# Attention levels as diagonal blocks in column tiles, and head outputs stored as two parts

## The chip, the cores and the metric

One program runs on one core of a Trainium2 chip. The metric is the time of one execution in device microseconds (us), the median of several runs; shorter is better.

## What is computed

The program is one inference step of a two-layer trunk on 1024 latent and 128 context tokens of width 1024, all in float32. Layer 0 mixes tokens by gated linear attention (4 heads, key width 128, value width 256, forward and backward), layer 1 by a Fourier mixer; each layer ends in a gated MLP with a width-3 convolution. The change touches the attention of layer 0 and the projection behind it. What that computes, from the reference:

```python
bcum = jnp.cumsum(gi, axis=2)
diff = bcum[:, :, :, None, :] - bcum[:, :, None, :, :]
decay = jnp.exp(jnp.where(lower[:, :, None], diff, -jnp.inf))
attn = jnp.einsum('bhik,bhjk,bhijk->bhij', qi, ki, decay)
o = (jnp.einsum('bhij,bhjv->bhiv', attn, vi)
     + jnp.einsum('bhik,bhkv->bhiv', qi * jnp.exp(bcum), state))
...
o = rmsnorm(o, norm_g) * jax.nn.silu(r.reshape(B, L, GLA_HEADS, GLA_DV))
return o.reshape(B, L, GLA_V) @ w_o, s_f, s_b
```

The decay between tokens i and j depends on the key channel, so `attn` is no plain product of queries and keys.

## The kernel before

The 1152 tokens lie along the free dimension, channels on the partitions, in three column groups of 384 (`CH`); each group has three chunks of 128 tokens. For every head and every group, in the order 2, 1, 0, `attention` builds the 128x128 matrices `A` (`att`) of the three chunks. It goes through seven levels with half block sizes s = 64, 32, 16, 8, 4, 2, 1 (`LEVELS`). At a level, the pairs (i, j) in the same block of 2s tokens but in different halves get their decay as a product of two factors that refer to the middle of the block: GpSimd (L535) and VectorE (L537) subtract the reference, ScalarE takes the exponential (L540), GpSimd multiplies the keys (L541), VectorE the queries (L546), all into one tile `le` of a pool with four buffers (tag `m3`). TensorE then multiplies for each of the three chunks all 128 keys with all 128 queries (L549), and VectorE takes from the result only the pairs of the level, by a predicated copy under a mask (L551). The diagonal comes from a plain product (L527) that ScalarE copies into `A` with factor 2 (L528). A product of two float32 operands is issued as two MATMUL instructions, each with a weight load.

The weights' projections (`pq`, `pk`, `pv`, `pr`, `wo`) are split: every operand is a float32r part and a rest, three products each (L97 to L99). A scheduler of the framework sets the order on every engine, from priorities and its own costs. The projections of the next head, and for the last head the first half of the output projection, have lower priority and so fill TensorE between the levels. `tick` puts products of the background modulation (`mods`, L175) behind levels 0, 2, 4 and 6: 32 stationary columns, four products side by side in four column tiles of the array.

The normed and gated output `r` of a group is stored to memory for heads 0 to 2 (L590). In the last head `load_ot` loads those of heads 0 and 1 group by group into buffers of the tag `wr`, which has two and serves the weights too (L607), and `split_ot` makes the two parts (ScalarE L601, VectorE L602) in pages of the tag `u`, of which there are 14. `w_out((0, 1), X)` then multiplies them with the weights `wo00` to `wo03` (L97 to L99), for every pair of output blocks over groups, then blocks. Head 2 is loaded behind the attention, and `w_out((2, 3), ...)` follows.

Of the kernel before, what the change touches and what calls it, by code (L numbers as in the profile page):

```python
# [24 lines left out]
P = 128  # L25
# [5 lines left out]
CH = 384  # L31
# [14 lines left out]
def trunk(tc, a, o):  # L46
# [21 lines left out]
    def at_ps(name):  # L68
        return pp.tile([P, 512], F32, tag="at", bufs=4, name=name)
# [312 lines left out]
    convb = const("convb", [P, 2, NF], src=a["convb"])  # L382
    mask = const("mask", [P, len(LEVELS), P], U8)
    mraw = sb.tile([P, 1032], F32, tag="wr", bufs=2, name="mraw")
    nc.sync.dma_start(mraw[:, :len(LEVELS) * P], a["mask"])
    V.tensor_copy(mask.rearrange("p l i -> p (l i)"), mraw[:, :len(LEVELS) * P])
    for ch in range(NCH):
        ev_glr(ch, pss[ch])

    ot_dram = [dr.tile([2, P, T], F32, name=f"ot{h}") for h in range(3)]  # L390

# [87 lines left out]
    def kv(kt, v, c):  # L479
# [3 lines left out]
        return ps  # L483

    def attention(h, qk, pages):

# [22 lines left out]
        for cg in (2, 1, 0):  # L509
# [13 lines left out]
            att = t15("A")  # L523
            ps = at_ps("lv")
            for c in range(3):
                s = cg * CH + c * P
                PE.matmul(ps[:, c * P:(c + 1) * P], lhsT=qk[:, s:s + P], rhs=qk[:, T + s:T + s + P], start=True, stop=True)  # L527
            S.activation(att, ps[:, :CH], AF.Copy, scale=2.0)  # L528
            for li, s in enumerate(LEVELS):
# [13 lines left out]
                else:  # L543
                    S.activation(e[:, 1], e[:, 1], AF.Exp, scale=1.0 / TAU)
                    kk, kb = qk, base
                V.tensor_tensor(e[:, 1], e[:, 1], qk[:, T + base:T + base + CH], op=ALU.mult)  # L546
                ps = at_ps("lv")
                for c in range(3):
                    PE.matmul(ps[:, c * P:(c + 1) * P], lhsT=view(kk, kb + c * P, [1, P]),  # L549
                              rhs=e[:, 1, c * P:(c + 1) * P], start=True, stop=True)  # L550
                ins = V.copy_predicated(att.rearrange("p (c i) -> p c i", i=P),  # L551
                                  mask[:, li, None, :].to_broadcast([P, 3, P]),
                                  ps[:, :CH].rearrange("p (c i) -> p c i", i=P))
                if li % 2 == 0:
                    tick(1, behind=ins)
            qb = t30("qb")
            S.activation(qb, bb.rearrange("p (z i) -> p z i", z=2), AF.Exp, scale=1.0 / TAU)
# [31 lines left out]
            if h < 3:  # L589
                nc.sync.dma_start(ot_dram[h][:, :, cols(cg)].rearrange("d p t -> p d t"),  # L590
                                  r.rearrange("p (d t) -> p d t", d=2))
            yield
# [10 lines left out]

    def load_ot(*hs):
        for cg, h in ((cg, h) for cg in range(3) for h in hs):
            raw = sb.tile([P, 1032], F32, tag="wr", bufs=2, name="otr")[:, :2 * CH].rearrange("p (d t) -> p d t", d=2)
            nc.sync.dma_start(raw, ot_dram[h][:, :, cols(cg)].rearrange("d p t -> p d t"))  # L607
            for d in range(2):
                split_ot(h, d, cg, raw[:, d])

    def w_out(hs, X, after=None):
# [13 lines left out]
        if not after:  # L625
            for m2 in range(4):
                whl = weight(a["gwo"][0, m2], 1024, f"wo0{m2}")
                for ch in range(NCH):
                    for mi in range(2):
                        block(2 * m2 + mi, ch, whl, mi)  # L630
            return
# [21 lines left out]
    for h in range(H):  # L653
# [5 lines left out]
        if h < 3:  # L659
            with later(LQ):  # L660
                qk = gla_qk(h + 1)
                ahead = gla_gates_v(h + 1, pages)
        else:
            finish()
            load_ot(0, 1)
        for cg in range(3):
# [891 lines left out]
```

## Time and profile before

| | us |
|---|---|
| median of 3 runs | 2561.12 (2558.16 to 2563.42) |
| the profiled execution | 2564.86 |
| span of its trace, first to last instruction | 2563.0 |

The trace counts an engine as busy while one of its instructions runs; matmuls overlap, and their ends are modelled, so the mean duration of one is longer than the distance between two. PE is TensorE's matmuls, PEld its weight loads, DVE VectorE, ACT ScalarE, POOL GpSimd, SP the engine whose queue issues most transfers. PEclk is TensorE's granted clock as a share of 2.4 GHz. The attention of layer 0 with its output projection lies between about 115 and 730 us of the span.

### The profile page before, as it was taken

How to read it: one execution, taken by the hardware profiler on the slowest of the kernel's cores; microseconds unless marked ns; L12 is line 12 of the kernel's file. 1: busy time of each engine (PE TensorE's matmuls, PEld its weight loads, DVE VectorE, ACT ScalarE, POOL GpSimd, SP SyncE). 2: the span in 40 equal slices, each digit the busy share in tenths (PEclk: the TensorE clock that was granted, in tenths of full speed). 3: DMA queues.
4: the chain of work that ended last, by engine and by line, in shares of the span. 5: the costliest groups of instructions: out<-in, count | busy, mean ns of one | idle time of the engine just before them, and what ended most of it. 6: DMA issues, size and time to landing. Idle time of an engine off the chain costs nothing. (4 is left out here: it accounts for less than half of the span.)

```text
span 2563.0 us, 46543 instructions
## 1 busy us (share of the span) xinstructions
PE 2425.1 (95%) x18122; PEld 2329.2 (91%) x18122; DVE 1841.2 (72%) x3339; ACT 1089.3 (43%) x2086; POOL 730.9 (29%) x548
## 2 busy tenths in 40 slices
PE   5999999987999999999999998999899999999997
PEld 4998988877999999999999996998899999999997
DVE  7647475566699677777787877277987778778676
ACT  5435344445364323333345564344533333334553
POOL 3435454453202333444100005230144444410000
PEclk8999999998999999999999999999999999999999
DMA  7212222204233453232674357344223232267334
GB/s 263 69 54 89 80 80 82 67 21 146 87 116 124 132 172 104 91 96 83 212 248 135 112 153 216 107 156 144 90 87 117 83 96 87 80 229 224 93 86 125
DMA packets 200972, 309.85 MB, mean 121 GB/s; under 512 B 18288, under 2 KB 142064, under 8 KB 200752
## 3 DMA queue, kind: packets, MB, share of 16 engines
q1 hardware_dynamic: 196528, 302.66, 37.2%
q10 hardware_dynamic: 4224, 4.23, 0.5%
q8 instruction: 142, 2.33, 0.4%
q14 instruction: 78, 0.64, 0.1%
HBM read 233.71 MB, written 73.11 MB: 120 GB/s over the span
## 5 line engine op out<-in xcount | busy, mean ns | idle before, releaser
L98 PE MATMUL pd<-hl,wd 128*128 128x288 f32 x1112 | 328.7, 299 | 5.4 <-DVE hl L1085 5.2
L99 PE MATMUL pd<-hh,wd 128*128 128x288 f32 x1112 | 326.7, 297 | 0.0
L97 PE MATMUL pd<-hh,wd 128*128 128x288 f32 x1112 | 316.5, 298 | 5.5 <-ACT hh L1084 3.2
L809 POOL TENSOR_TENSOR s<-wa,s 128x512 fp32r<-128x512 f32 x114 | 157.0, 1377 | 278.6 <-ACT s L808 278.6
L1084 ACT ACTIVATE hh<-hr 128x288 fp32r<-128x288 f32 x308 | 133.2, 437 | 222.1 <-PE pd L98 213.3
L98 PEld LDWEIGHTS pd<-hl,wd 128*128 128x128 f32 x1112 | 210.8, 190 | 7.9 <-DVE hl L1085 7.4
L1085 DVE TENSOR_TENSOR hl<-hr,hh 128x288 fp32r<-128x288 f32 x308 | 138.5, 455 | 109.3 <-ACT hh L1084 108.7
L97 PEld LDWEIGHTS pd<-hh,wd 128*128 128x128 f32 x1112 | 204.2, 188 | 10.8 <-ACT hh L1084 5.7
L99 PEld LDWEIGHTS pd<-hh,wd 128*128 128x128 f32 x1112 | 210.4, 190 | 0.0
L809 POOL TENSOR_TENSOR a<-wa,a 128x512 fp32r<-128x512 f32 x76 | 100.1, 1318 | 334.7 <-ACT a L808 231.1
L808 ACT ACTIVATE s<-wa 128x512 fp32r<-128x512 f32 x120 | 75.5, 630 | 189.8 <-DVE wa L826 116.1
L977 ACT ACTIVATE hid<-hid 128x576 f32<-128x576 f32 x88 | 60.4, 686 | 161.5 <-DVE hid L972 102.0
L1074 DVE TENSOR_TENSOR wd<-wd,wd 128x512 fp32r<-128x512 f32 (+1 forms) x184 | 116.4, 642 | 9.7 <-ACT wd L1073 4.9
L808 ACT ACTIVATE a<-wa 128x512 fp32r<-128x512 f32 x80 | 50.3, 631 | 141.0 <-PE pa L99 76.2
L1073 ACT ACTIVATE wd<-wd 128x512 fp32r<-128x512 f32 (+1 forms) x184 | 104.4, 580 | 11.7 <-PE ps L99 4.0
L860 DVE TENSOR_TENSOR q<-q,ps 128x288 f32<-128x288 f32 x232 | 98.4, 444 | 10.1 <-PE ps L99 8.4
L535 POOL TENSOR_TENSOR le<-vbr 128x384 f32<-128x384 f32 x72 | 74.0, 1032 | 109.3 <-PE lv L549 95.5
L1208 POOL TENSOR_TENSOR fn<-fn 128x512 f32<-128x512 f32 x8 | 14.1, 1764 | 312.9 <-ACT wp L728 293.3
L541 POOL TENSOR_TENSOR le<-le,qk 128x384 f32<-128x384 f32 x72 | 91.6, 1278 | 35.6 <-ACT le L540 34.7
L97 PE MATMUL pa<-fh1x,a 128*128 128x288 f32 x320 | 95.3, 298 | 5.9 <-DVE c L860 3.6
L97 PE MATMUL ps<-fh1x,s 128*128 128x288 f32 x320 | 95.2, 298 | 3.0 <-DVE hid L917 3.0
L97 PE MATMUL ps<-fh0t,s 128*128 128x288 f32 x320 | 96.4, 302 | 1.4 <-DVE c L860 1.4
(689 smaller groups left out, 8852.5 us busy)
## 6 DMA issues: line engine op xcount, KB each, us to landing
hr<-hid SPq DMA_DIRECT2D x308, 144.0 KB, 2.2
wm<-in_wmod SPq DMA_DIRECT2D x112, 256.0 KB, 2.9
hid<-hid SPq DMA_DIRECT2D x44, 576.0 KB, 3.8
wa<-in_wup SPq DMA_DIRECT2D x40, 512.0 KB, 3.5
wg<-in_wup SPq DMA_DIRECT2D x40, 512.0 KB, 4.1
hid<-t SPq DMA_DIRECT2D x132, 144.0 KB, 3.3
wd<-in_wdn SPq DMA_DIRECT2D x16, 1024.0 KB, 8.0
wm<-in_wmod SPq DMA_DIRECT2D x96, 128.0 KB, 3.5
```

The source lines that it names most:

```text
L97: PE.matmul(ps, lhsT=wh, rhs=xh, start=first, stop=False, skip_group_check=skip)
L98: PE.matmul(ps, lhsT=wh, rhs=xl, start=False, stop=False, skip_group_check=skip)
L99: PE.matmul(ps, lhsT=wl, rhs=xh, start=False, stop=last, skip_group_check=skip)
L535: G.tensor_tensor(view(e, 0, [2 * s, nb], [s, 2], [1, s]), ref, view(bb, 0, [2 * s, nb], [CH + s, 2], [1, s]), op=ALU.subtract)
L541: G.tensor_tensor(e[:, 0], e[:, 0], qk[:, base:base + CH], op=ALU.mult)
L808: S.activation(w[name][:, :512], x, AF.Copy)
L809: (eng or G).tensor_tensor(w[name][:, 512:], x, w[name][:, :512].bitcast(F32), op=ALU.subtract)
L860: add.last = V.tensor_tensor(out[:, xs], x[:, xs], ps[s][:, :SUB], op=op)
L1073: S.activation(hi, x, AF.Copy)
L1074: low = V.tensor_tensor(lo, x, hi.bitcast(F32), op=ALU.subtract)
L1084: S.activation(hi[:, c], raw, AF.Copy)
L1085: V.tensor_tensor(lo[:, c], raw, hi[:, c].bitcast(F32), op=ALU.subtract)
```

## The change

Level 64 stays three full products, which ScalarE copies into `A`. Level 32 is computed only in diagonal blocks of 64, two column tiles a chunk; levels 16 to 1 and the diagonal only in diagonal blocks of 32, four column tiles a chunk (`diagonal`). Per column group that is 3 products of 128 columns, 6 of 64 and 72 of 32, in the place of 24 of 128. The products are issued in groups: level 64; levels 32, 16 and the diagonal; levels 8 and 4; levels 2 and 1. The blocks of 32 are gathered in a tile `near` of 96 columns by predicated copies, and four copies put it into `A`.

The outputs of heads 0 to 2 are split where they are made, over their values `v` and in place, and both parts are stored; `load_ot` loads a page of a head and half in one transfer from GpSimd's queue, without a split and without a buffer of `wr`. In the first `w_out` the loop over blocks is now outside that over groups.

```diff
--- before.py
+++ after.py
@@ -380,14 +380,18 @@
     gng = const("gng", [P, 2], src=a["gng"])
     convw = const("convw", [P, 2, 3, NF], src=a["convw"])
     convb = const("convb", [P, 2, NF], src=a["convb"])
-    mask = const("mask", [P, len(LEVELS), P], U8)
+
+    mask = const("mask", [P, len(LEVELS) - 2, 32], U8)
     mraw = sb.tile([P, 1032], F32, tag="wr", bufs=2, name="mraw")
     nc.sync.dma_start(mraw[:, :len(LEVELS) * P], a["mask"])
-    V.tensor_copy(mask.rearrange("p l i -> p (l i)"), mraw[:, :len(LEVELS) * P])
+    for g in range(4):
+        b = slice(32 * g, 32 * g + 32)
+        V.tensor_copy(mask[b], mraw[b, 2 * P:len(LEVELS) * P].rearrange("p (l i) -> p l i", i=P)[:, :, b])
     for ch in range(NCH):
         ev_glr(ch, pss[ch])
 
-    ot_dram = [dr.tile([2, P, T], F32, name=f"ot{h}") for h in range(3)]
+
+    ot_dram = [dr.tile([2, P, 2, T], F32, name=f"ot{h}") for h in range(3)]
 
     VV, BB, RR = slice(0, 2 * CH), slice(2 * CH, 4 * CH), slice(4 * CH, 6 * CH)
 
@@ -481,6 +485,14 @@
         PE.matmul(ps[:, :256], lhsT=kt[:, (c % 3) * P:(c % 3 + 1) * P], rhs=v[:, (c % 3) * 256:(c % 3 + 1) * 256],
                   start=True, stop=True)
         return ps
+
+    def diagonal(ps, n, kk, at, q):
+
+        for c in range(3):
+            for g in range(P // n):
+                PE.matmul(ps[n * g:n * g + n, c * n:(c + 1) * n], lhsT=view(kk, at + c * P + n * g, [1, n]),
+                          rhs=q[:, c * P + n * g:c * P + n * g + n], start=True, stop=True,
+                          **({} if n == P else dict(tile_position=(0, n * g))))
 
     def attention(h, qk, pages):
 
@@ -521,11 +533,9 @@
                     sbs[c - 1] = s_n
 
             att = t15("A")
-            ps = at_ps("lv")
-            for c in range(3):
-                s = cg * CH + c * P
-                PE.matmul(ps[:, c * P:(c + 1) * P], lhsT=qk[:, s:s + P], rhs=qk[:, T + s:T + s + P], start=True, stop=True)
-            S.activation(att, ps[:, :CH], AF.Copy, scale=2.0)
+            att3 = att.rearrange("p (c i) -> p c i", i=P)
+            near = sb.tile([P, 96], F32, tag="near", bufs=2, name="near")
+            todo = []
             for li, s in enumerate(LEVELS):
                 nb = CH // (2 * s)
                 base = cg * CH
@@ -543,16 +553,41 @@
                 else:
                     S.activation(e[:, 1], e[:, 1], AF.Exp, scale=1.0 / TAU)
                     kk, kb = qk, base
-                V.tensor_tensor(e[:, 1], e[:, 1], qk[:, T + base:T + base + CH], op=ALU.mult)
-                ps = at_ps("lv")
-                for c in range(3):
-                    PE.matmul(ps[:, c * P:(c + 1) * P], lhsT=view(kk, kb + c * P, [1, P]),
-                              rhs=e[:, 1, c * P:(c + 1) * P], start=True, stop=True)
-                ins = V.copy_predicated(att.rearrange("p (c i) -> p c i", i=P),
-                                  mask[:, li, None, :].to_broadcast([P, 3, P]),
-                                  ps[:, :CH].rearrange("p (c i) -> p c i", i=P))
+                made = V.tensor_tensor(e[:, 1], e[:, 1], qk[:, T + base:T + base + CH], op=ALU.mult)
+                todo.append((li, max(2 * s, 32), kk, kb, e[:, 1]))
+                ins = made
+                if li % 2 == 0:
+                    ps = at_ps("lv")
+                    at = 0
+                    with tc.issue_after(made.ins):
+                        for lj, n, kk, kb, q in todo:
+                            diagonal(ps[:, at:], n, kk, kb, q)
+                            at += 3 * n
+                        if li == 2:
+                            diagonal(ps[:, at:], 32, qk, base, qk[:, T + base:T + base + CH])
+                            S.activation(near, ps[:, at:at + 96], AF.Copy, scale=2.0)
+                    at = 0
+                    for lj, n, *_ in todo:
+                        src = ps[:, at:at + 3 * n].rearrange("p (c i) -> p c i", i=n)
+                        at += 3 * n
+                        if n == P:
+                            ins = S.activation(att3, src, AF.Copy)
+                        elif n == 64:
+                            S.activation(att3[:64, :, :64], src[:64], AF.Copy)
+                            ins = V.tensor_copy(att3[64:, :, 64:], src[64:])
+                        else:
+                            ins = V.copy_predicated(near.rearrange("p (c i) -> p c i", i=32),
+                                                    mask[:, lj - 2, None, :].to_broadcast([P, 3, 32]), src)
+                    todo = []
                 if li % 2 == 0:
                     tick(1, behind=ins)
+            for g in range(4):
+                b = slice(32 * g, 32 * g + 32)
+                src = near[b].rearrange("p (c i) -> p c i", i=32)
+                if g % 2:
+                    S.activation(att3[b, :, b], src, AF.Copy)
+                else:
+                    V.tensor_copy(att3[b, :, b], src)
             qb = t30("qb")
             S.activation(qb, bb.rearrange("p (z i) -> p z i", z=2), AF.Exp, scale=1.0 / TAU)
             V.tensor_tensor(qb, qb, view(qk, T + cg * CH, [0, 2], [1, CH]), op=ALU.mult)
@@ -587,8 +622,13 @@
                     V.tensor_tensor(o1, o1, rv, op=ALU.mult)
                     split_ot(3, d, cg, o1)
             if h < 3:
-                nc.sync.dma_start(ot_dram[h][:, :, cols(cg)].rearrange("d p t -> p d t"),
-                                  r.rearrange("p (d t) -> p d t", d=2))
+
+                hi = v.bitcast(F32R)
+                S.activation(hi, r, AF.Copy)
+                V.tensor_tensor(r.bitcast(F32R), r, hi.bitcast(F32), op=ALU.subtract)
+                for i, x in enumerate((v, r)):
+                    nc.sync.dma_start(ot_dram[h][:, :, i, cols(cg)].rearrange("d p t -> p d t"),
+                                      x.rearrange("p (d t) -> p d t", d=2))
             yield
 
     ots = {}
@@ -601,12 +641,10 @@
         S.activation(hi, src, AF.Copy)
         V.tensor_tensor(lo, src, hi.bitcast(F32), op=ALU.subtract)
 
-    def load_ot(*hs):
-        for cg, h in ((cg, h) for cg in range(3) for h in hs):
-            raw = sb.tile([P, 1032], F32, tag="wr", bufs=2, name="otr")[:, :2 * CH].rearrange("p (d t) -> p d t", d=2)
-            nc.sync.dma_start(raw, ot_dram[h][:, :, cols(cg)].rearrange("d p t -> p d t"))
-            for d in range(2):
-                split_ot(h, d, cg, raw[:, d])
+    def load_ot(h):
+        for d in range(2):
+            ots[h, d] = page(f"ot{h}{d}", F32R)
+            nc.gpsimd.dma_start(ots[h, d], ot_dram[h][d].rearrange("p i t -> p (i t)"))
 
     def w_out(hs, X, after=None):
         gate = vec(0, 2)
@@ -625,8 +663,8 @@
         if not after:
             for m2 in range(4):
                 whl = weight(a["gwo"][0, m2], 1024, f"wo0{m2}")
-                for ch in range(NCH):
-                    for mi in range(2):
+                for mi in range(2):
+                    for ch in range(NCH):
                         block(2 * m2 + mi, ch, whl, mi)
             return
         ws = []
@@ -662,7 +700,8 @@
                 ahead = gla_gates_v(h + 1, pages)
         else:
             finish()
-            load_ot(0, 1)
+            load_ot(0)
+            load_ot(1)
         for cg in range(3):
             next(att)
             if h < 3:
```

What this moves, at three places. In the rows, `lv` are the levels' results, `le` the factors, `mods` the background's, `pv` a projection of the next head; x3 is three like it.

TensorE, second column group of head 0, before, from the background's products behind level 16 to level 4 (the two rows x3 of `lv` are levels 8 and 4):

```order
L175 MATMUL mods_1856<-wm_1826,cs 32x128 x4
L175 MATMUL mods_1856<-wm_1828,cs 32x128 x4
L549 MATMUL lv<-le 128x128 x3
L98 MATMUL pv_1727<-wv10l,h_303 128x256
L99 MATMUL pv_1727<-wv10h,h_303 128x256
L97 MATMUL pv_1727<-wv10h,h_304 128x256
L98 MATMUL pv_1727<-wv10l,h_304 128x256
L99 MATMUL pv_1727<-wv10h,h_304 128x256
L97 MATMUL pv_1727<-wv10h,h_305 128x256
L549 MATMUL lv<-le 128x128 x3
L98 MATMUL pv_1727<-wv10l,h_305 128x256
```

and now, from level 64 to level 4 (the last row):

```order
L493 MATMUL lv<-le 128x128 x3
L493 MATMUL lv<-le 64x64 x6
L493 MATMUL lv<-le 32x32 x9
L186 MATMUL mods_1578<-sel,mrow_1891 128x8
L493 MATMUL lv<-le 32x32 x3
L493 MATMUL lv<-qk_689 32x32 x12
L493 MATMUL lv<-le 32x32
L175 MATMUL mods_1942<-wm_1887,cs 32x128 x4
L175 MATMUL mods_1942<-wm_1889,cs 32x128 x4
L493 MATMUL lv<-le 32x32 x11
L98 MATMUL pv_1792<-wv10l,h_303 128x256
L493 MATMUL lv<-le 32x32 x12
```

The products of levels 32 to 8 now stand together with the background's eight, one row of the projection `pv` stands between levels 8 and 4 where six stood, and a full product of the background (L186) stands inside level 16.

TensorE, last column group of the last head, with the output projection `wo` of heads 0 and 1 as the filling, before:

```order
L549 MATMUL lv<-le 128x128
L97 MATMUL wo_5503<-ot_5150,wo01h 128x384
L549 MATMUL lv<-le 128x128
L98 MATMUL wo_5503<-ot_5150,wo01h 128x384
L549 MATMUL lv<-le 128x128
L99 MATMUL wo_5503<-ot_5150,wo01l 128x384
L97 MATMUL wo_5503<-ot_5153,wo01h 128x384
L98 MATMUL wo_5503<-ot_5153,wo01h 128x384
L99 MATMUL wo_5503<-ot_5153,wo01l 128x384
L97 MATMUL wo_5524<-ot_5142,wo02h 128x384
```

and now:

```order
L493 MATMUL lv<-le 128x128 x3
L493 MATMUL lv<-le 64x64 x6
L493 MATMUL lv<-le 32x32 x11
L98 MATMUL wo_6204<-ot_5701,wo03h 128x384
L493 MATMUL lv<-le 32x32
L99 MATMUL wo_6204<-ot_5701,wo03l 128x384
L493 MATMUL lv<-qk_4264 32x32
L97 MATMUL wo_6204<-ot_5703,wo03h 128x384
L493 MATMUL lv<-qk_4264 32x32
L98 MATMUL wo_6204<-ot_5703,wo03h 128x384
L493 MATMUL lv<-qk_4264 32x32
L99 MATMUL wo_6204<-ot_5703,wo03l 128x384
```

Full products of a level alternated with the filling before; now products of a single 32-column tile do, one by one.

GpSimd, the last head's first two column groups (`ke` are the keys for the states, L87 the rest of a weight), before:

```order
L471 TENSOR_TENSOR ke<-ke,qk_3889 128x384
L87 TENSOR_TENSOR wr31l<-wr_4990,wr31h 128x1024
L471 TENSOR_TENSOR ke<-ke,qk_3889 128x384 x3
L535 TENSOR_TENSOR le<-vbr_4264 128x384 x2
L541 TENSOR_TENSOR le<-le,qk_3889 128x384 x2
L535 TENSOR_TENSOR le<-vbr_4558 128x384 x3
L541 TENSOR_TENSOR le<-le,qk_3889 128x384 x3
```

and now:

```order
L87 TENSOR_TENSOR wo01l<-wo_6014,wo01h 128x1024
L545 TENSOR_TENSOR le<-vbr_5057 128x384
L551 TENSOR_TENSOR le<-le,qk_4264 128x384
L647 DMA ot_5703<-ot_686 128x2304
L647 DMA ot_5705<-ot_687 128x2304
L87 TENSOR_TENSOR wo02l<-wo_6106,wo02h 128x1024
L647 DMA ot_5707<-ot_687 128x2304
L545 TENSOR_TENSOR le<-vbr_5057 128x384
L545 TENSOR_TENSOR le<-vbr_5368 128x384
L551 TENSOR_TENSOR le<-le,qk_4264 128x384 x2
```

The transfers of the pages `ot` stand in GpSimd's own order among the factors of the levels.

## Rows read from the trace of the kernel before

**Rows 1.** The page's first part: busy time, share, instructions

```profile
PE 2425.1 (95%) x18122; PEld 2329.2 (91%) x18122; DVE 1841.2 (72%) x3339; ACT 1089.3 (43%) x2086; POOL 730.9 (29%) x548
```

**Rows 2.** Busy time by stretch: stretch, length, engines (xcount), PEclk, DMA share, GB/s

```profile
115.60:257.00 141.40, 131.59 (x998) 119.66 (x995) 80.73 (x128) 59.40 (x104) 62.12 (x48) 1.00 0.26 80
...
594.00:616.00 22.00, 10.62 (x37) 8.88 (x36) 14.95 (x21) 13.72 (x22) 11.42 (x7) 0.61 0.58 206
616.00:730.00 114.00, 112.03 (x659) 109.73 (x658) 77.14 (x152) 38.09 (x69) 16.67 (x9) 0.99 0.30 106
```

**Rows 3.** Waits of PE, 115.6 to 534.8 us: total, times, longest

```profile
PE kt L474 <- POOL ke L471: 10.1, 9, 2.9
PE ov L577 <- DVE os L575: 5.5, 9, 1.6
PE mods L175 <- DMA wm<-in_wmod: 4.4, 3, 2.1
```

**Rows 4.** Waits of PE, 534.8 to 730 us

```profile
PE wo L97 <- ACT wo00h L86: 7.0, 1, 7.0
PE ov L577 <- DVE os L575: 6.5, 3, 2.9
PE o L565 <- DVE A L551: 2.5, 1, 2.5
PE wo L99 <- POOL wo00l L87: 1.4, 1, 1.4
```

**Rows 5.** Timeline, PE, 545 to 551 us: start, length, idle before it

```profile
545.20 2.84 PE L549 MATMUL lv<-le 128*128 128x128 f32 x24
549.94 0.91 PE L549 MATMUL lv<-le 128*128 128x128 f32 x6 [0.67 <-DVE le L546]
```

**Rows 6.** Timeline, PE, 130.9 to 136 us

```profile
131.00 0.65 PE L175 MATMUL mods<-wm,cs 128*32 128x128 f32 x16
...
134.93 0.28 PE L549 MATMUL lv<-le 128*128 128x128 f32 x1
135.13 0.42 PE L175 MATMUL mods<-wm,cs 128*32 128x128 f32 x8
135.49 0.44 PE L99 MATMUL pr<-h,wr00l 128*128 128x384 f32 x1
135.77 0.34 PE L97 MATMUL pr<-h,wr00h 128*128 128x384 f32 x1
135.94 0.33 PE L98 MATMUL pr<-h,wr00h 128*128 128x384 f32 x1
```

**Rows 7.** Line 175 alone, busy time by stretch of hundredths of a us

```profile
135.12:135.16 0.04, 0.03 (x4) 0.03 (x5) 1.00 0.00 0
135.16:135.26 0.10, 0.10 (x4) 0.10 (x8) 1.00 0.00 0
135.26:135.30 0.04, 0.04 (x8) 0.03 (x4) 1.00 1.75 410
```

**Rows 8.** Timeline, PE, end of the span: six products with 96 weight columns

```profile
2551.64 0.67 PE L256 MATMUL var<-mean,acc 128*96 128x2 f32 x6 [3.13 <-DVE acc L235]
```

**Rows 9.** Timeline, the other engines, 546 to 549 us

```profile
546.12 1.93 POOL L535 TENSOR_TENSOR le<-vbr 128x384 f32<-128x384 f32 x2 [7.84 <-PE lv L549]
547.45 0.84 ACT L540 ACTIVATE le<-le 128x768 f32<-128x768 f32 x1 [1.50 <-DVE le L537]
548.37 2.28 POOL L541 TENSOR_TENSOR le<-le,qk 128x384 f32<-128x384 f32 x2 [0.33 <-ACT le L540]
548.86 0.93 DVE L546 TENSOR_TENSOR le<-le,qk 128x384 f32<-128x384 f32 x1
```

**Rows 10.** Groups by line and shape, DVE, whole span: busy us, mean ns

```profile
L551 DVE COPY_PREDICATED A<-mask,lv 128x384 f32<-128x384 uint8 x84 | 49.2, 586 | 12.5 <-PE lv L549 7.5 <-ACT mrow L184 5.0
L624 DVE SCALAR_TENSOR_TENSOR x<-wo,modT,x 128x384 f32<-128x384 f32 x32 | 19.6, 614 | 16.7 <-PE wo L99 16.3 <-DMA x<-in_xT 0.3
L558 DVE TENSOR_TENSOR qb<-qb,qk 128x768 f32<-128x768 f32 x12 | 12.4, 1034 | 0.0
L602 DVE TENSOR_TENSOR ot<-otr,ot 128x384 fp32r<-128x384 f32 x18 | 11.0, 637 | 6.2 <-ACT ot L601 6.2
L624 DVE SCALAR_TENSOR_TENSOR x<-wo,modT,x 128x128 f32<-128x128 f32 x16 | 5.5, 343 | 0.0
```

**Rows 11.** Timeline, the norm of an attention output, 561 to 566 us

```profile
561.69 0.54 DVE L575 TENSOR_TENSOR os<-os,os 128x384 f32<-128x384 f32 x1
564.48 1.14 DVE L582 SCALAR_TENSOR_TENSOR o<-o,gng,os 128x384 f32<-128x384 f32 x2 [1.18 <-ACT os L579]
```

**Rows 12.** DMA issues, 520 to 740 us: KB each, median us to landing

```profile
x<-in_xT SPq DMA_DIRECT2D x4, 1152.0 KB, 8.6
```

## The prediction

> **What bounds the kernel now.** I read the busy shares first: TensorE 95%, VectorE 72%, the others under half [rows 1]. Then the busy time by stretch: in the attention TensorE works 131.6 of 141.4 us in the stretch of head 0, VectorE 80.7; only between 594 and 616 us TensorE rests, 10.6 busy of 22.0, at a granted clock of 0.61 [rows 2]. So TensorE's time is the stage's time, plus its waits. They come to about 25 us from 115.6 to 534.8 us, most of them for the keys of the states and for the norm [rows 3], and 18.9 us behind that, of which 8.4 are for the first weight of the output projection [rows 4]. The timelines show what a level costs and what it waits for [rows 5, 9], and what a change to column tiles and back costs, since the background's products already use them [rows 6, 7]. All sums are made against the profiled execution, 2564.9 us; the median of the three runs is 3.7 us lower.
>
> **Products of the levels.** Eighteen more level instructions take 2.84 - 0.91 us [rows 5], 0.107 each; a product is two, 0.214. A column group has 24: 5.15 us. Now it has 3 of these (0.64), 6 of 64 columns and 72 of 32. For 64 by 64 I take half the columns and two tiles side by side, 0.054: 0.32 us. For 32 by 32 the nearest row is the background, 32 weight columns but 128 moving: eight more instructions take 0.65 - 0.42 us [rows 6], 0.029 each, 0.058 a product. That is the upper end, and at it a group costs 5.14 us and nothing is saved. At the lower end only a quarter of the columns streams, 0.0145. The weights allow it: six loads of 96 columns with 2 moving ones take 0.67 us in all [rows 8], at most 0.037 us for 32 columns, and four tiles load side by side. Four products start within 0.04 us and no other in the next 0.10 [rows 7], so a start costs 0.01 at most and the 0.11 from four to four is streaming. I take 0.015: 1.08 us. A group then costs 2.04, saving 3.1; twelve groups (4 heads by 3) save **37.3**, ends 0 and 37.
>
> The Trainium skill (TensorE: Matmul & The Clock Gate, section "Wait — 56ns, not 53.3ns?") says that starts never come closer than about 25 ns however few columns there are. Taken across the tiles, 144 instructions would need 3.6 us a group, by estimate 30 us more over twelve groups; four starts in 0.04 us [rows 7] speak against it between tiles.
>
> **Changes of the array's mode.** From the last full product to the second projection row behind eight tiled ones it is 135.77 - 134.93 = 0.84 us; the work in it is 0.107, 8 by 0.029 and 0.17 (the distance 135.77 to 135.94) [rows 6]. The rest, **0.33 us**, is there and back: the array empties twice and loads weights without cover. I counted the runs of tiled products in TensorE's order up to the end of the output projection: 48 before, 183 now. Of the 135 more, 50 are in heads 0 to 2, and the last head has 75 that are one single level product between two rows of filling (the second place of the change). 135 by 0.33 is **44.6**. The ends are 0.30 and 0.37 a time, 40 and 50.
>
> No row shows a lone 32-column product. The Trainium skill (TensorEngine Tiling (Array Packing), section "Key Properties") has every change of tiling mode drain the array, however little is done between; by it single products pay like groups, and the sum is the one I make.
>
> Singles also lose the company of other tiles: 25 background products now stand alone, 0.214 for 0.058, 3.9 us; 75 level products take an estimated 0.06 for 0.015, 3.4; and eleven direct turns from 64 to 32 columns at half a trip are 1.9. Together **9.2**. TensorE's own work thus grows by 44.6 + 9.2 - 37.3 = **16.5**.
>
> **The chain of the levels.** Four buffers hold the factors, so those of level 4 start when level 64's products end: 545.20 + 0.91 = 546.11, GpSimd at 546.12; two subtractions, the exponential, GpSimd's and VectorE's products, and TensorE starts at 549.94, 3.8 us later, after 0.67 idle [rows 5, 9]. Without the predicated copies ahead of VectorE's part GpSimd bounds it: 1.93 + 1.14 + 0.3, 3.4 us. TensorE's work in between is now, for the first place shown: 6 by 0.054, 36 by 0.015, eight background products at 0.058, two trips, half a trip in, half a turn's worth from 64 to 32, and two full rows, about 2.5 us (2.0 to 2.8 over ten groups). So it waits 0.8 to 0.9 in each of ten groups; some 2 us of such waits exist now. **+6**, ends 0 and 13.
>
> **VectorE.** Seven predicated copies of 0.586 leave, 4.1 us a group. By the line through 0.614 at 384 and 0.343 at 128 columns, 0.31 stands for 96 and 0.41 for 192 [rows 10]: five copies, one of 192 and two of 96 are 2.6. Twelve groups save 18 us, 18 splits of 0.637 go (11.5), nine subtractions of 768 columns at 1.034 come (9.3). Twenty us less on an engine that TensorE waits for behind the norm and the state keys [rows 3]: I take **-4**, ends 0 and -12. ScalarE's changes (copies, nine more of 768 columns, 18 splits fewer) stay under its 43% and are set at nothing; were it the last to finish, nine copies of under 1 us would show. The nine more stores lie under a DMA share of 0.26 [rows 2]; the next head's state load queues behind them on SP, where VectorE has time.
>
> **The last head.** The loads leave the two `wr` buffers, so the weights no longer queue behind them: 7.0 + 1.4 go, and the wait of 2.5 for `A` too, as 19 rows of filling instead of 5 stand behind the last level of that group [rows 4]. A clock of 0.61 is 78% of that stretch at 1.2 GHz, some 8.2 of the 10.6 busy us; at 2.4 GHz they are 4.1 less [rows 2]. **-15**, ends 0 and -17.
>
> The filling of the first projection now ends with the last level of the last group. Before, that stretch is 112.0 of 114.0 us busy [rows 2]. The norm takes 561.69 to 565.62, 3.9 us, from its sum to its last product [rows 11], and gating and splitting about 1 more, with little beside it: **+5**, ends 0 and 8.
>
> **Sum:** 16.5 + 6 - 4 - 15 + 5 = +8.5, 2573.4 for a profiled execution, **2570** for the median.
>
> **The rivals.** A, faster: VectorE's queue is what TensorE's waits hang on. With 20 us less there, level 4 finds its factors (0 for +6), the waits for norm and state keys shrink by 12, the end is covered (0 for +5) and the last head gives 17: 16.5 - 12 - 17 = -12.5, **2549**. For it: VectorE is named in the wait before level 4 [rows 5]; against: GpSimd's three steps alone are 3.4 us. It decides when level 4 starts under 2.8 us behind level 64.
>
> B: small tiles run no faster than the background's, 0.058 a product: 37.3 more, less the 6 of the chain, **2601**. Against it stands the burst of four [rows 7]. The skill's floor between starts, named above, would come near this.
>
> C: the pages come late. Three wait for the last projections that read the old pages, and GpSimd and the levels queue behind their issue. Some 22 lone products with filling, 0.54 us each, cover 12 us, and the filling of the first page 5 more; a page of that size lands after 8.6 us [rows 12], three in turn after 26: 9 us of wait, **2579**.
>
> D: the lone products leave the array so idle that its clock falls to 1.2 GHz, as it did in the stretch at 0.61 [rows 2]. Some 75 times 0.23 us of array work doubles, 17 us, **2587**. Against it: runs of background products stand at a clock of 1.00 [rows 7].
>
> **How the numbers follow.** Forecast 0.48, A 0.24, C 0.13, D 0.08, B 0.07. Under 0.2%, 5 us, no measurement of this kernel tells a change. The forecast's terms spread it over 2558 to 2582: 0.30 slower, 0.16 same, 0.02 faster. A gives 0.20 faster and 0.04 same; C, D and B are slower. Together faster 0.22, same 0.20, slower 0.58. The range 2548 to 2590 leaves out B and the lower half of A.
>
> **What would show it.** Right: runs of tiled products with 0.2 us on either side, four 32-column instructions in about 0.03 us, alternating stretches in the last head of 0.5 to 0.6 us a step; a wait of 0.5 to 1.5 us before level 4; no wait for `wo00`; an idle gap before the second projection. Wrong: tiled products between full ones without the 0.33 us, or level 4 without a wait, would turn the sign; a wait on the loads of `ot` or a clock under 1 in the last head would add.

## The result, and the profile after

The changed kernel takes 2593.64 us (median of four runs, 2592.51 to 2601.66) against 2561.3 us; the ratio is 1.0134, interval 1.0111 to 1.0157. The forecast had the side right, 2570 us, and the loss nearly four times too small (8.9 us for 32.3); 2593.6 lies above the range. The profiled execution took 2601.66 us, 36.8 more than that of before; the stretches below are of these two executions. The page's first part now, as [rows 1]:

```profile
PE 2446.8 (94%) x19490; PEld 2317.3 (89%) x19490; DVE 1840.6 (71%) x3345; ACT 1096.0 (42%) x2123; POOL 736.9 (28%) x554
```

VectorE works as long as before, 1840.6 us for 1841.2, though some 20 us were reckoned to leave it. Where the time went is read from stretches cut at each head's first product of the projection `pr` and at the last of `wo` (columns as in [rows 2], which has head 0 before, 141.4 us). Before, heads 1, 2 and 3:

```profile
257.00:397.00 140.00, 133.09 (x1011) 120.51 (x1010) 79.59 (x127) 60.32 (x104) 64.00 (x50) 0.99 0.26 81
397.00:534.80 137.80, 128.61 (x942) 117.88 (x941) 78.93 (x127) 60.10 (x104) 60.50 (x46) 0.99 0.21 66
534.80:729.60 194.80, 175.89 (x1035) 167.83 (x1034) 132.94 (x237) 81.07 (x136) 56.62 (x42) 0.94 0.27 93
```

Now, heads 0 to 3:

```profile
115.10:263.70 148.60, 133.10 (x1337) 117.69 (x1334) 85.95 (x132) 63.82 (x119) 60.50 (x47) 0.94 0.27 84
263.70:409.70 146.00, 131.82 (x1353) 115.27 (x1352) 84.78 (x133) 64.39 (x119) 63.01 (x49) 0.98 0.29 86
409.70:553.40 143.70, 129.58 (x1293) 114.44 (x1291) 85.66 (x134) 64.26 (x117) 63.34 (x50) 0.98 0.24 73
553.40:764.90 211.50, 197.32 (x1373) 169.69 (x1372) 116.58 (x224) 74.43 (x129) 59.53 (x46) 0.96 0.29 102
```

These four hold 35.8 of the 36.8 us: 19.1 in heads 0 to 2, 16.7 in the last. In heads 0 to 2 TensorE stands idle 43.8 us instead of 25.9, and is busy 394.5 us instead of 393.3, more of it than before at the lower of its two clocks, 1.2 GHz: the granted clock is 0.94, 0.98 and 0.98 where it was 1.00, 0.99 and 0.99. Its waits in heads 0 to 2, for [rows 3]:

```profile
PE lv L493 <- DVE le L556: 12.5, 7, 2.4
PE kt L478 <- POOL ke L475: 9.4, 9, 1.7
PE mods L175 <- DVE modT L187: 7.7, 7, 1.8
PE ov L612 <- DVE os L610: 5.4, 9, 0.8
...
PE lv L493 <- POOL le L551: 1.3, 2, 0.7
```

The first, on the factors of a level, was this one before:

```profile
PE lv L549 <- DVE le L546: 1.1, 3, 0.5
```

The third, on `modT`, and the last are new; the second and fourth stayed. One group shows how they arise, TensorE first (the last row of the fence is level 4):

```profile
197.24 1.64 PE L493 MATMUL lv<-le 128*128 128x128 f32 x36
...
200.62 0.64 PE L175 MATMUL mods<-wm,cs 128*32 128x128 f32 x16 [1.03 <-DVE modT L187]
201.09 0.37 PE L493 MATMUL lv<-le 128*32 128x32 f32 x22
201.38 0.38 PE L98 MATMUL pv<-wv10l,h 128*128 128x256 f32 x1
203.35 0.40 PE L493 MATMUL lv<-le 128*32 128x32 f32 x24 [1.59 <-DVE le L556]
```

and VectorE and GpSimd in the same stretch:

```profile
198.18 2.31 DVE L547 TENSOR_TENSOR le<-vbr 128x384 f32<-128x384 f32 x2
200.42 0.15 DVE L187 TENSOR_TENSOR modT<-mods,bmod 128x8 f32<-128x8 f32 x1
200.49 1.44 DVE L547 TENSOR_TENSOR le<-vbr 128x384 f32<-128x384 f32 x1
201.85 1.36 DVE L556 TENSOR_TENSOR le<-le,qk 128x384 f32<-128x384 f32 x1
```

```profile
198.16 1.93 POOL L545 TENSOR_TENSOR le<-vbr 128x384 f32<-128x384 f32 x2 [3.50 <-PE lv L493]
200.41 2.39 POOL L551 TENSOR_TENSOR le<-le,qk 128x384 f32<-128x384 f32 x2 [0.33 <-ACT le L550]
```

Level 4 starts 203.35 - 197.24 = 6.11 us after level 64's first product; before it was 549.94 - 545.20 = 4.74 [rows 5], and 4.74 in the group shown here as well. Two things stretch it: level 1's subtraction (1.44) stands ahead of level 4's query product, and VectorE's instructions run long exactly while GpSimd's do, 1.36 us where 0.93 stood [rows 9].

A run of tiled products is what stands between two full ones, and a trip the change from full to tiled products and back. In the last head single products alternate with the filling (timeline; a row of filling by itself is 0.17 from the next [rows 6]):

```profile
602.36 0.25 PE L493 MATMUL lv<-le 128*32 128x32 f32 x2
602.54 0.44 PE L98 MATMUL pr<-h,wr31h 128*128 128x384 f32 x1
602.91 0.25 PE L493 MATMUL lv<-le 128*32 128x32 f32 x2
603.08 0.44 PE L99 MATMUL pr<-h,wr31l 128*128 128x384 f32 x1
```

A period is 603.08 - 602.54 = 0.54 us, so a trip costs about 0.35: the period less the 0.17, and less some 0.015 for the product itself.

### The profile page after: what moved, and what is told of

Same layout as the page of the kernel before. It is cut to its first block, busy times and chain, and to the rows that moved or that the text cites. A ratio compares the mean times of both kernels' runs of the same rounds, so it can differ in the third digit from the quotient of the medians.

```text
span 2599.9 us, 49329 instructions
## 1 busy us (share of the span) xinstructions
PE 2446.8 (94%) x19490; PEld 2317.3 (89%) x19490; DVE 1840.6 (71%) x3345; ACT 1096.0 (42%) x2123; POOL 736.9 (28%) x554
## 3 DMA queue, kind: packets, MB, share of 16 engines
q1 hardware_dynamic: 196528, 302.66, 36.8%
## 5 line engine op out<-in xcount | busy, mean ns | idle before, releaser
L899 DVE TENSOR_TENSOR c<-q,pa 128x288 f32<-128x288 f32 x80 | 36.0, 450 | 89.1 <-PE pa L99 85.6
```

The lines of the kernel that those rows point to most:

```text
L899: add.last = V.tensor_tensor(out[:, xs], x[:, xs], ps[s][:, :SUB], op=op)
```

## The experiments

**The two parts apart.** The changed kernel with the old stores, `load_ot` and loop of `w_out`:

```diff
-            load_ot(0)
-            load_ot(1)
+            load_ot(0, 1)
```

> Only the levels are changed; outputs of heads are stored, loaded and split as before, with the old loop order in the first output projection. Theory (the levels carry the loss: trips, the wait before level 4, the wait on modT, the clock): slower than before by 25 to 40 us, with the stretch of each of the heads 0 to 2 still 6 to 7 us longer than before. Rival (the pages that come late are what was missed): slower than before by only 5 to 15 us.

2603.3 us, ratio 1.0165 (1.015 to 1.018), 41.6 us slower than before: slightly above the theory. With the outputs as well (2593.64) it is 9.7 less. And the outputs alone, on the old levels:

> Only the outputs of heads 0 to 2 are changed (two parts, six page loads on GpSimd's queue, other loop order); levels as before. Theory, by my sum (the weights no longer queue behind the loads): faster than before by 5 to 15 us, the waits of 7.0 and 1.4 us for wo00 gone. Rival (late pages): 0 to 10 us slower, with waits for a page ot in their place.

2556.83 us, ratio 0.9982 (0.9968 to 0.9995): a gain of 4.8 us, just under the theory's lower end. The waits for `wo00` are gone, but in the last stretch (191.2 us for 194.8) others stand there:

```profile
PE kt L474 <- POOL ke L471: 5.3, 3, 3.0
PE wo L97 <- ACT vbr L449: 3.9, 1, 3.9
```

The loss is the levels'.

**Late filling.**

```diff
-                with later(LV):
+                with later(2400):
                     w_out((0, 1), X)
```

> The changed kernel with a lower priority for the first output projection, so that the level products of the last head stand in groups: 51 runs of tiled products fewer in TensorE's order. Theory (0.30 us a trip): 13 to 18 us faster than the changed kernel. Rival (alternating costs little, the filling is missed later): within 5 us of the changed kernel, or slower.

2588.95 us, ratio 1.01 (1.0073 to 1.0127): 4.7 less by the medians, as the rival had it, but 13.0 by the profiled executions. The last stretch is 199.2 us instead of 211.5. TensorE is busy 180.6 us there instead of 197.3, 0.33 us less for each of the 51 runs, and waits 4.4 us more. The price of a trip is borne out; the total does not decide between the two.

**VectorE's order.**

```diff
+                with tc.issue_after(mades[li - 2].ins) if li > 4 else ExitStack():
```

around the subtraction of line 547, `mades` being the list of the levels' `made`.

> The changed kernel with VectorE's subtraction of levels 2 and 1 held behind its query product of two levels before, so level 1's subtraction no longer stands ahead of level 4's product. Theory (VectorE's order makes the wait before level 4): level 4 starts about 4.2 us behind level 64's last product instead of 5.56 in the groups of heads 0 to 2, that wait falls from 12.5 us in all to under 4, and the kernel is 8 to 16 us faster than the changed one, the low clock behind that wait included. Rival (GpSimd's pace or the shared access of GpSimd and VectorE sets it): the wait stays over 10 us or moves to levels 2 and 1, the time within 4 us of the changed kernel.

2586.87 us, ratio 1.011 (1.0083 to 1.0137), 6.8 less; heads 0 to 2 fell by 13.1 us (145.4, 141.8, 138.0). Of these, 9.6 are TensorE's busy time (384.9 us for 394.5, with the clock at 0.96, 1.00 and 0.99) and only 3.5 its idle time. The same group's rows:

```profile
197.67 1.63 PE L493 MATMUL lv<-le 128*128 128x128 f32 x36
...
202.41 0.42 PE L493 MATMUL lv<-le 128*32 128x32 f32 x24 [0.52 <-DVE le L557]
```

Level 4 starts 4.74 us behind level 64, the old distance to the hundredth. The theory holds for that distance and nearly for the waits before the levels (5.1 us in all now, for under 4); the gain of the kernel stayed under its 8 us; the waits on GpSimd's factors rose from 1.3 to 3.9 us.

**Each wait taken away by itself moves.** A bank for the background's result:

```diff
-                pt = ps[:, P:P + 8]
+                pt = at_ps("modt")[:, :8]
```

> The changed kernel, with the background's small transposed result in a bank of its own, so that the next background products no longer wait until VectorE has read it. Theory (these waits are a loss of their own): the 7.7 us of waits on modT in heads 0 to 2 are gone, 11 runs of tiled products fewer save 3 us more, and the kernel is 7 to 12 us faster than the changed one. Rival (VectorE paces the levels anyway): the time goes into the wait before level 4, which stands right behind; within 4 us of the changed kernel.

2623.09 us, ratio 1.0237 (1.0195 to 1.028): a miss, worse than either theory. The waits on `modT` are gone and those before the levels more than doubled; levels 32 to 4 now stand in one piece, the row of filling ahead of level 4 gone:

```profile
PE lv L493 <- DVE le L556: 29.8, 15, 2.9
```

> The three repairs together: late filling, VectorE's order, a bank for the background's result. Theory (each loss stands for itself): gains add up, 4.7 + 6.8 + about 8 us against the changed kernel, about 2574 us. Rival (they share one cause, VectorE's queue): no more than the larger two, 2582 us or above.

2615.13 us (1.0199, 1.0156 to 1.0242): nothing adds up while the bank is in it.

**Fewer trips.** Each group's tiled products in two runs:

```diff
-                if li % 2 == 0:
+                if li in (0, 3, 6):
...
+                        todo = [todo[2], todo[3], todo[1], todo[0]]
...
+                        with tc.issue_after(lead.ins) if lead else ExitStack():
```

> The changed kernel with each column group's tiled products in two runs: levels 32, 16, 8 and the diagonal, and levels 4, 2 and 1, the last level's factors first in each, and the background's products beside them; VectorE's order and the late filling as in the experiments before. The runs of tiled products up to the end of the output projection fall from 183 to about 55. Theory (a trip costs 0.30 us wherever it stands): the time from full to tiled products and back falls by about 35 us, the stage is shorter than in the kernel before, the kernel at 2550 to 2568 us. Rival (what counts is the chain of the factors; with level 1's first, TensorE waits longer in one piece): waits before the second run of 2 us or more a group take most of it back, 2575 to 2595 us.

2588.66 us (1.0099, 1.0063 to 1.0134), as the rival had it. Head 0 took 138.3 us, under the 141.4 of before, heads 1 and 2 took 150.9 and 149.4. The products end together, so what hangs on the last comes late:

```profile
PE o L610 <- DVE A L600: 18.8, 9, 3.5
PE kt L478 <- POOL ke L475: 15.1, 9, 5.7
```

Then level 64 ahead of the states' keys, so that the chain starts early:

```diff
-            kt = khat(qk, bb, 1, cg)
...
+                if li == 1:
+                    kt = khat(qk, bb, 1, cg)
```

> The changed kernel, with level 64 of a group computed ahead of the keys for the states, so that its buffer comes free early and the factors of level 4 are made under the projection; in TensorE's order level 64 stands dozens of rows ahead of level 32. 30 runs of tiled products fewer as well. Theory (the loss of heads 0 to 2 is the chain of the factors behind level 64, with the clock that falls in its waits): waits before level 4 fall from 12.5 us to under 4, the stretches of heads 0 to 2 come to 141 us or less each, and the kernel is 15 to 25 us faster than the changed one. Rival (any wait removed comes back before the next level, since VectorE and GpSimd slow each other down): less than 8 us faster.

2601.79 us (1.0125, 1.0092 to 1.0159): no gain. With the order and the late filling:

> The same with VectorE's order and the late filling: 88 runs of tiled products fewer than in the changed kernel. Theory (chain and trips are separate losses): 2555 to 2568 us. Rival (they are the same loss): no better than the kernel with level 64 first alone, within 4 us of it.

2587.08 us (1.0085, 1.0058 to 1.0111). With two runs a group:

> Level 64 first, and the tiled products in two runs a group. Theory (with the chain out of the way the streaming that the tiles save is left over, 9 us a head by the accounts of the two-run kernel): 2540 to 2560 us. Rival (the second run waits for level 1 and the copies of A wait for it, as in the two-run kernel): 2570 to 2590 us.

2577.24 us (1.0048, 1.0034 to 1.0063), as the rival had it, 18.4 us of it in waits for the states' keys from GpSimd. Removing trips and placing levels helps, but GpSimd's and VectorE's work comes late wherever TensorE is sent.

**VectorE alone.** The key halves of levels 4 and 2 on VectorE (level 1 has none); `True` for `s <= 4` moves all:

```diff
-                    G.tensor_tensor(e[:, 0], e[:, 0], qk[:, base:base + CH], op=ALU.mult)
+                    (V if s <= 4 else G).tensor_tensor(e[:, 0], e[:, 0], qk[:, base:base + CH], op=ALU.mult)
```

and the same on line 545.

> The changed kernel with the key halves of levels 4 and 2 (subtraction and product) on VectorE instead of GpSimd. Theory (the two engines slow each other: a subtraction or product of VectorE takes 0.55 us without GpSimd's work beside it and about 1.0 to 1.2 with it): though VectorE has four more instructions a group, its subtractions fall from a mean of 0.97 us towards 0.8, level 4 starts 4.0 to 4.8 us behind level 64 instead of 5.56, and the kernel is 4 to 12 us faster than the changed one. Rival (VectorE's load is what counts): level 4 starts later than now, the kernel is 5 to 15 us slower.

2595.39 us (1.0123, 1.0092 to 1.0154), no gain, though the waits before the levels fell to 2.3 us in heads 0 to 2; 14.1 stand at the states' keys, 5.3 at `kv` and 7.4 at the copies of `A`. On the kernel with level 64 first and two runs:

> Level 64 first and two runs a group, with the key halves of levels 4 and 2 on VectorE. Theory: GpSimd's keys for the states come earlier too, their waits fall from 18.4 us to under 10, the time to 2560 to 2570 us. Rival: 2577 us or more, as without it.

2586.77 us (1.0095, 1.007 to 1.012), 9.5 slower than without: a miss. All levels:

> The same with all levels' key halves on VectorE, GpSimd only making the keys for the states. Theory (the slowing of each other is most of what GpSimd's share saves): VectorE's mean for a subtraction and a product falls to about 0.6 us, the waits for the keys of the states nearly go, the time 2550 to 2570 us. Rival (VectorE becomes the bound of the attention): heads 0 to 2 take 150 us or more each, 2590 us or above.

2558.13 us (0.9971, 0.9952 to 0.999), as the theory had it. On the old levels, half and all:

> The outputs in two parts with the old full-width levels, and the key halves of levels 4 and 2 on VectorE. Theory (the waits for the keys of the states, 6.4 us in heads 0 to 2, hang on GpSimd's queue): 3 to 6 us faster than the outputs alone, about 2552 us. Rival (with the predicated copies of 0.59 us VectorE has no room): slower than the outputs alone by 3 to 10 us.

> Outputs in two parts, the old full-width levels, all levels' key halves on VectorE: what the tiles are worth when VectorE has the work alone. Theory (the predicated copies of 384 columns leave VectorE no room): 5 us or more slower than the outputs alone, so that the diagonal blocks pay only here. Rival (GpSimd's help is worth nothing with the old levels either): as fast as the outputs alone or faster, 2545 to 2557 us.

2578.93 us (1.006, 1.0036 to 1.0083) and 2559.97 us (0.9998, 0.9985 to 1.0011), against 2556.83 for the outputs alone, 22 and 3 us slower: the first is worse than its rival, the second under its theory's 5 us. Full-width levels gain nothing from it. The states' keys on VectorE as well (line 475, `G` to `V`), beside level 64 first and two runs:

> Level 64 first, two runs a group, all levels on VectorE, and the keys for the states on VectorE too. Theory (the 17.3 us of waits for these keys come from GpSimd, whose queue holds weight splits of 2.4 to 3.0 us ahead of them): these waits fall under 8 us, the time is 4 to 10 us less than with the keys on GpSimd, about 2550 us. Rival (VectorE is full now): within 3 us of it or slower.

2546.52 us (0.9939, 0.9923 to 0.9954): faster than both kernels. The waits for the keys fell less than hoped, from 13.9 to 8.8 us in heads 0 to 2.

**The changed kernel, VectorE alone, nothing else:**

> The changed kernel with all levels' key halves on VectorE and nothing else. It has 34 runs of tiled products more in its order than the changed kernel, most of them single products in the last head. Theory (meeting of VectorE and GpSimd makes the waits of heads 0 to 2): each of these heads takes 5 us or more less than in the changed kernel, level 4 starts under 4.5 us behind level 64, the time is 8 to 20 us less, the trips of the last head excepted. Rival (two runs and level 64 first made the gain of the run before): within 5 us of the changed kernel or slower.

2590.71 us (1.0107, 1.0083 to 1.013). The total is that of the rival and hides two opposite moves:

```profile
116.90:255.50 138.60, 130.46 (x1334) 114.51 (x1331) 79.59 (x161) 60.52 (x111) 15.80 (x9) 0.96 0.27 85
255.50:393.30 137.80, 129.32 (x1352) 114.37 (x1351) 88.31 (x170) 64.25 (x120) 22.92 (x13) 0.98 0.29 91
393.30:527.80 134.50, 126.38 (x1288) 111.78 (x1287) 86.83 (x170) 64.08 (x119) 22.80 (x13) 0.99 0.24 78
527.80:756.20 228.40, 212.30 (x1379) 173.97 (x1378) 132.77 (x260) 78.50 (x137) 33.05 (x21) 0.97 0.28 98
```

Heads 0 to 2 fell from 438.3 to 410.9 us, below the 419.2 of before and by over 8 us each, as the theory had it; the last head grew to 228.4, where the trace now has 126 runs of tiled products for 85. So the late filling was added, and nothing else:

> The changed kernel with two edits that leave its products and their levels' order alone: all levels' key halves on VectorE, and the late filling, which takes 116 single runs of tiled products out of the last head. Theory (meeting of VectorE and GpSimd costs heads 0 to 2, trips cost the last head, and the two add up): heads 0 to 2 as in the run with VectorE alone, 411 us in all, the last head at 200 us or less instead of 228, the time 2558 to 2568 us, so the loss of the change is gone. Rival (the trips are not what makes the last head long): the last head stays over 215 us, 2580 us or more.

2547.97 us, ratio 0.9946 (0.9925 to 0.9966). The last stretch:

```profile
524.80:712.90 188.10, 171.78 (x1383) 160.30 (x1382) 133.35 (x257) 76.67 (x136) 33.43 (x21) 0.95 0.34 119
```

228.4 - 188.1 = 40.3 us for 116 runs, 0.35 a trip. Two edits that leave every product as the change has it turn the loss into a gain of 14 us by the ratio. Faster than the theory, too: heads 0 to 2 came to 407.7 us. The old levels with VectorE alone stand at 0.9998, but no run has them with the late filling, so the totals do not compare. In heads 0 to 2, which the late filling leaves alone, they took 423.0 us against the 410.9 of the run before: there the diagonal blocks pay.

One more thing moved in these last two runs, though no edit names it: what the scheduler sets between the levels. The same group in the last experiment:

```profile
194.89 1.63 PE L493 MATMUL lv<-le 128*128 128x128 f32 x36
...
197.58 0.37 PE L493 MATMUL lv<-le 128*32 128x32 f32 x22
197.88 0.39 PE L98 MATMUL pv<-wv10l,h 128*128 128x256 f32 x1
...
199.41 0.28 PE L98 MATMUL pv<-wv11l,h 128*128 128x256 f32 x1
199.73 0.40 PE L493 MATMUL lv<-le 128*32 128x32 f32 x24
```

Thirteen rows of the projection stand between levels 8 and 4 where one stood, and 12 for 2 on average in the nine groups of heads 0 to 2. Level 4 starts 199.73 - 194.89 = 4.84 us behind level 64, no sooner than in the kernel before. So TensorE's wait there is gone as much by the work set in front of it as by a shorter chain. The filling alone does not do it: with half of the levels on VectorE the same 12 rows stand there, and heads 0 to 2 still took 435.3 us.

## Why the prediction failed

**The streaming was right.** 24 instructions of level 4 last 0.40 us, 0.2 of it the last one's own: 0.017 a product for the 0.015 taken. **The trips were right** in number and price, 0.35 for 0.33. Together these two terms and the side of the forecast stand, and rival B falls.

**The step that failed is "VectorE, -4", and with it "the chain of the levels, +6".** Level 4's chain was to shrink from 3.8 to 3.4 us; from GpSimd's first subtraction to level 4 it is 203.35 - 198.16 = 5.2. The copies were costed by their busy time, as if any 18 us off VectorE were relief. Groups by line and shape (busy us, mean ns), before:

```profile
L546 DVE TENSOR_TENSOR le<-le,qk 128x384 f32<-128x384 f32 x84 | 72.1, 870 | 12.4 <-ACT le L540 11.4 <-ACT le L544 0.9
L537 DVE TENSOR_TENSOR le<-vbr 128x384 f32<-128x384 f32 x84 | 63.1, 764 | 11.1 <-PE o L570 11.0
```

now:

```profile
L547 DVE TENSOR_TENSOR le<-vbr 128x384 f32<-128x384 f32 x84 | 80.0, 969 | 20.9 <-PE o L605 14.5 <-PE lv L493 5.7
L556 DVE TENSOR_TENSOR le<-le,qk 128x384 f32<-128x384 f32 x84 | 75.2, 917 | 8.8 <-ACT le L550 8.7
```

and with VectorE alone, in the last experiment:

```profile
L547 DVE TENSOR_TENSOR le<-vbr 128x384 f32<-128x384 f32 x84 | 50.2, 603 | 0.0
L556 DVE TENSOR_TENSOR le<-le,qk 128x384 f32<-128x384 f32 x84 | 46.1, 552 | 0.2
```

The same instruction takes 0.55 us alone and up to 1.4 beside the levels' work on GpSimd. Of the 168 in two such rows, 20 meet no instruction of GpSimd before and 22 now, and these last 0.54 to 0.56 us. The predicated copies do not lengthen, though 77 of the 84 run beside GpSimd's work: their shortest, median and longest before are

```profile
L551 DVE COPY_PREDICATED A<-mask,lv x84: 572/584/608, 129.2 to 650.5; 128x384 f32<-128x384 uint8 x84
```

They were the one part of VectorE's work on the levels that ran beside GpSimd's at no cost, and they stood between the others. By the starts and ends in the two traces, GpSimd's work lay over these copies for 44.7 us before and over those in their place for 11.8 now; over the subtractions and products it lay for 97.6 us and now for 117.1. No more of them meet it (146 for 148), but they meet it for longer. That is the 20 us more in these two rows, and the relief is gone. The Trainium skill (SBUF — State Buffer, section "SBUF: two separate sides") says why: a VectorE instruction with two inputs in SBUF and a GpSimd instruction that reads SBUF take a shared pair of ports for their whole length, one after the other. The traces agree: the query product of 1.36 us in the fence above is 0.55 and some 0.8 more while GpSimd's products run (to 202.80), and a predicated copy, with its data in PSUM, is not slowed. The prediction took the lengths in [rows 9] for these instructions' own.

So the waits before the levels and on `modT` came to 12.5 + 7.7 + 1.3 (on GpSimd) in heads 0 to 2 and 1.9 in the last, 23 us instead of 2, where +6 was forecast. The bound of 3.4 us for level 4's chain also took VectorE's order as it was: with the copies gone the scheduler put level 1's subtraction ahead, and 4.7 us became 6.1. With the order put back it is 4.74 again and the waits on VectorE's factors fall from 12.5 us to 5.1, so more than half of them is the order's. But 4.74 is not less than before: the copies' leaving did not shorten the chain, which fits the longer instructions. The wait on `modT` was not foreseen at all.

**The clock** was put at nothing in heads 0 to 2. The missing share of it times the length of each stretch is, as an estimate from the rows above, 15 us now and 3 before, so it cost 12. TensorE's own work there then fell by some 11 us, about what the sum had for these heads (9 groups at 3.1 saved, 50 trips at 0.33 paid). The 19.1 us are 18 of waits and 12 of the clock, less these 11.

**The last head** came near its sum, 16.7 us for some 12 (85 trips, three groups saved, 75 single products, and the 10 below), but not by its terms: -15 + 5 stood for the outputs and the end, and the outputs gave 3.6 us in that stretch on the old levels and 3.9 beside the tiled ones (211.5 for 215.4). The 8.4 us for `wo00` became other waits. So most of the 28 us that the forecast missed by lie in heads 0 to 2.

Of the **rivals**, A named the right engine and the wrong sign: 20 us less did not arrive. C came in part (5.3 us for a page of `ot` in the last head). D came in the other place: heads 0 to 2 stand at 0.94, 0.98 and 0.98, with stretches like this one, most of it at 1.2 GHz, behind the 1.59 us of waiting shown above:

```profile
204.20:208.20 4.00, 4.00 (x74) 3.08 (x73) 3.99 (x7) 0.00 (x0) 2.63 (x3) 0.57 0.12 20
```

In the last experiment they stand at 0.99, 0.98 and 0.97, some 8 us by the same estimate, so of the 30.6 us that it gains in heads 0 to 2 about 7 are the clock's.

**Left open:** why half of the levels on VectorE brings nothing where all bring 27 us in heads 0 to 2; and how much of that gain is VectorE's shorter instructions, how much that the chain no longer passes through GpSimd's own 0.8 to 1.3 us steps, and how much the filling that the scheduler now sets ahead of level 4. The runs change all three together. That the two engines slow each other is shown; that this alone makes TensorE's waits is argued.

## What to carry to other kernels

Work removed from an engine is relief only where that work was in the way: ask what its neighbours do in the gap, and whether two engines now do the same kind of work at the same time. Read an instruction's own length from its shortest occurrence, not from one with another engine's work beside it. And count changes of the array's mode in the scheduled order: here each trip cost about 0.35 us, for one product between full rows (0.35) as for eight (0.33).

## What was not expected of the hardware

In the last experiment VectorE, without GpSimd's help at the levels, has 144 instructions more than in the changed kernel, 83 us of them, and works only 17 us longer over the whole span, 1857.6 us for 1840.6; the attention is faster. GpSimd's share of the factors cost VectorE most of what it took off it. With the old full-width levels the same move gained nothing.
